# HGRN2 and RG-LRU layer: masked score copies over 64 rows, and two copies given to ACT

## The chip, the cores and the metric

One core of a Trainium2 chip runs the whole kernel. The metric is the device time of one execution in microseconds. The engines are named as in the profile: PE (TensorE, matmuls) with its weight loads PEld, DVE (VectorE), ACT (ScalarE), POOL (GpSimd) and SP (SyncE, which issues the transfers).

## The reference

One layer of a hybrid decoder over 2048 tokens of width 1024, all in float32. After an RMS norm, one input projection feeds two mixers side by side: HGRN2 (4 heads, 128x128 state each, chunks of 32 tokens) and RG-LRU (width 512). Their outputs are concatenated and projected back; then come a SwiGLU feed-forward part (inner width 2816) and a last RMS norm. The parts that the change touches are these:

```python
def step(state, xs):                       # HGRN2, one chunk of 32
    q_, k_, lg, v_ = xs
    b = jnp.cumsum(lg, axis=-2)
    q_dec = q_ * jnp.exp(b)
    k_dec = k_ * jnp.exp(-b)
    scores = jnp.where(causal, jnp.einsum('bhtk,bhsk->bhts', q_dec, k_dec), 0.0)
    o = jnp.einsum('bhts,bhsv->bhtv', scores, v_) + jnp.einsum('bhtk,bhkv->bhtv', q_dec, state)
    k_state = k_ * jnp.exp(b_last - b)
    new_state = jnp.exp(b_last)[..., 0, :, None] * state + jnp.einsum('bhsk,bhsv->bhkv', k_state, v_)
...
log_a = -LRU_C * r * jax.nn.softplus(-a_param)      # RG-LRU
a = jnp.exp(log_a)
b_in = jnp.sqrt(-jnp.expm1(2.0 * log_a)) * (ig * xc)
```

## The kernel before

The tokens go through in two halves of 1024, and each half in two column blocks (c = 0, 1) of 512. Every float32 operand of a large matmul is split into a high and a low part, and a product is three matmuls (high by high, low by high, high by low). The high part is made by ACT, the low part by DVE.

For each half there is first the projection of the values (`pv`), then eight steps s, then the gate projection (`pg`), the output projection (`poh`), and later the feed-forward part (`quad`, `pda`, `pdb`). A step s takes two slices of the input projection, computes them for both column blocks by 24 matmuls each (`pa`, `pb`, lines 234 to 236), and is of the HGRN2 kind where s is even (one head) and of the RG-LRU kind where s is odd. So a half has 8 HGRN2 units and 8 RG-LRU units, the whole kernel 16 of each, in pairs: two HGRN2 units, two RG-LRU units, and so on.

A HGRN2 unit has three parts.

- `hg_pre` (lines 252 to 319) takes `pa` and `pb` and prepares the decayed queries and keys. On ACT: two sigmoids (lines 254, 255), a logarithm (257), exponentials (262, 278 to 280). On DVE: a scan over each chunk (259) and some twenty products, of which lines 310, 315 and 318 are among the last. 128 tokens are treated as one block of four chunks of 32.
- `hg_mid` (322 on) is put behind the next unit's `pa`. PE transposes the state keys into the bank `pk` (329), DVE copies them to `kut` (331), PE forms the scores of each block in the bank `pc` (337), rows 0 to 63 by the columns 0 to 127 and rows 64 to 127 by the columns 64 to 127. The scores are copied to `sct`, a tile that was zeroed once and whose lower triangle stays zero: on the diagonal 32x32 pieces by DVE, under a mask (`keep`, 349), right of them by ACT (351). PE then forms the state update `pu` from `kut` (354), and DVE adds it to the states (359).
- `hg_post` is put behind the unit after that: PE forms the outputs `po` from the states (371) and from the scores (372), ACT sums their squares (377), POOL takes the power -0.5 (379), and DVE scales (380).

A RG-LRU unit has `lru_pre` (copy, GELU on ACT at 391, a convolution on DVE at 397 and 401, the split at 207 and 208) and `lru_post`: PE forms the two gates `pr` and `pi` (411 to 413), ACT their sigmoids (416, 417), a tanh (419) and the decay `r` by Exp (420); DVE squares `r` into `xc` (422) and combines it with the tanh (423), ACT takes the root (424), and DVE goes on with a product (425), the scan (426) and the gating (428). The next step's weights are split in between (163, 164).

Tiles come from pools with few slots. The banks `pk`, `pc`, `pu`, `po`, `pr` and `pi` share four of the eight PSUM banks; `kut`, the states `S` and the gates' tiles share the five slots of `late`.

The order of the work on each engine is not written out by hand. The program says what depends on what, and with

```python
with tile.TileContext(nc, schedule_with_timeline_sim=True) as tc:
```

a planner puts all instructions into one queue for each engine when the program is built, with a model of the instructions' times. On the chip each engine takes its queue in order. The loads of activation tables on ACT (`ACT_TABLE_LOAD` in the profile) are put in ahead of the functions that need them.

Of the kernel before, what the change touches and what calls it, by code (L numbers as in the profile page):

```python
# [10 lines left out]
AF = mybir.ActivationFunctionType  # L11
ALU = mybir.AluOpType

P = 128
# [11 lines left out]
TPC = CW // P  # L26
NTT = T // P
SUB = 32
# [7 lines left out]
def hybrid_layer(ctx: ExitStack, tc: tile.TileContext, x, x_t, norm_w, cols, w_in, gate_w, w_out, w_gu, w_down, out):  # L36
    nc = tc.nc
    const = ctx.enter_context(tc.tile_pool(name="const", bufs=1))
# [24 lines left out]
    def late(nm):  # L63
        return sb.tile([P, CW], F32, tag="late", name=nm, bufs=5)
# [4 lines left out]
    def aux(nm):  # L69
        return psp.tile([P, CW], F32, tag="aux", name=nm)  # L70
# [4 lines left out]
    mask = const.tile([P, CW], mybir.dt.bfloat16, name="mask")  # L75
    nc.gpsimd.memset(mask, 1.0)
    nc.gpsimd.memset(mask.rearrange("p (n s) -> p n s", s=SUB)[:, :, 0:1], 0.0)

    keep = const.tile([P, SUB], mybir.dt.uint8, name="keep")
    tri = sb.tile([P, CW], F32, tag="pg", name="tri", bufs=16)  # L80
    nc.gpsimd.memset(tri, 1.0)
    nc.gpsimd.affine_select(
        out=tri[:, 0:P], in_=tri[:, 0:P], pattern=[[1, P]], compare_op=ALU.is_ge, fill=0.0, base=0, channel_multiplier=-1
    )
    for j in range(4):
        nc.gpsimd.tensor_copy(out=keep[j * SUB : (j + 1) * SUB], in_=tri[j * SUB : (j + 1) * SUB, j * SUB : (j + 1) * SUB])
    sc_t = []
    for i in range(2):
        s = const.tile([P, TPC, P], F32, name=f"sct{i}")
# [8 lines left out]
    v = nc.vector  # L98
# [225 lines left out]
    def hg_mid(h, c, st, vt, nm):  # L324
        hs = slice(h * P, (h + 1) * P)
        W, Wy, K, KU, G = (st[k] for k in ("W", "Wy", "K", "KU", "G"))
        pk = aux("pk" + nm)
        for n in range(TPC):
            nc.tensor.transpose(out=pk[:, n * P : (n + 1) * P], in_=KU[:, n * P : (n + 1) * P], identity=ident)
        kut = late("kut" + nm)  # L330
        v.tensor_copy(out=kut, in_=pk)

        pc = aux("pc" + nm)
        for n in range(TPC):
            o = n * P
            for r0, w in ((0, W), (2 * SUB, Wy)):
                nc.tensor.matmul(
                    pc[r0 : r0 + 2 * SUB, o + r0 : o + P],
                    lhsT=K[:, o + r0 : o + r0 + 2 * SUB],
                    rhs=w[:, o + r0 : o + P],  # L340
                    start=True,
                    stop=True,
                )
        sc = sc_t[flip[0] % 2]
        flip[0] += 1
        pc4 = pc.rearrange("p (n t) -> p n t", t=P)
        for j in range(4):
            rows, cs = slice(j * SUB, (j + 1) * SUB), slice(j * SUB, (j + 1) * SUB)
            v.copy_predicated(out=sc[rows, :, cs], mask=keep[rows].unsqueeze(1).broadcast_to([SUB, TPC, SUB]), data=pc4[rows, :, cs])
            if j < 3:  # L350
                nc.scalar.copy(out=sc[rows, :, (j + 1) * SUB : P], in_=pc4[rows, :, (j + 1) * SUB : P])
        pu = aux("pu" + nm)
        for n in range(TPC):
            nc.tensor.matmul(pu[:, n * P : (n + 1) * P], lhsT=kut[:, n * P : (n + 1) * P], rhs=vt[:, n, hs], start=True, stop=True)

        S = late("S" + nm)
        states = [carry[:, c % 2, h, :]] + [S[:, n * P : (n + 1) * P] for n in range(TPC - 1)] + [carry[:, 1 - c % 2, h, :]]
        for n in range(TPC):
            v.scalar_tensor_tensor(
                out=states[n + 1], in0=states[n], scalar=G[:, n, 3:4], in1=pu[:, n * P : (n + 1) * P], op0=ALU.mult, op1=ALU.add  # L360
            )
        st["S"], st["sc"] = states, sc
# [22 lines left out]
    def lru_pre(u, psx, psg, nm):  # L385
        xp = sb.tile([P, CW + 4], F32, tag="pg", name="xp" + nm, bufs=16)
        v.tensor_copy(out=xp[:, 0:3], in_=hist[:, u, :])
        nc.scalar.copy(out=xp[:, 3 : 3 + CW], in_=psx)
        nc.gpsimd.tensor_copy(out=hist[:, u, :], in_=xp[:, CW : CW + 3])
        gl = page("gl" + nm)  # L390
        nc.scalar.activation(out=gl, in_=psg, func=AF.Gelu_apprx_tanh)
        xc = page("xc" + nm)

        def cw(k):
            return par[:, C_CONVW + k * 4 + u : C_CONVW + k * 4 + u + 1]

        v.tensor_scalar(
            out=xc, in0=xp[:, 0:CW], scalar1=cw(0), scalar2=par[:, C_CONVB + u : C_CONVB + u + 1], op0=ALU.mult, op1=ALU.add
        )
        for k in range(1, 4):  # L400
            v.scalar_tensor_tensor(out=xc, in0=xp[:, k : k + CW], scalar=cw(k), in1=xc, op0=ALU.mult, op1=ALU.add)
        xh, xl = page("xh" + nm, dt=F32R), page("xl" + nm, dt=F32R)
        split((xh, xl), xc)
        return gl, xc, xh, xl


    def lru_post(u, gl, xc, xh, xl, y, nm):
        pr, pi = aux("pr" + nm), aux("pi" + nm)
        for m, pg in enumerate((pr, pi)):
            gs = slice((m * NU + u) * P, (m * NU + u + 1) * P)  # L410
            nc.tensor.matmul(pg, lhsT=gwh[:, gs], rhs=xh, start=True, stop=False)
            nc.tensor.matmul(pg, lhsT=gwl[:, gs], rhs=xh, start=False, stop=False)
            nc.tensor.matmul(pg, lhsT=gwh[:, gs], rhs=xl, start=False, stop=True)
        r, ig, t = late("r" + nm), late("ig" + nm), late("t" + nm)
        us = slice(u, u + 1)
        nc.scalar.activation(out=r, in_=pr, func=AF.Sigmoid, bias=par[:, C_BA + u : C_BA + u + 1])
        nc.scalar.activation(out=ig, in_=pi, func=AF.Sigmoid, bias=par[:, C_BX + u : C_BX + u + 1])

        nc.scalar.activation(out=t, in_=r, func=AF.Tanh, scale=msp[:, us])
        nc.scalar.activation(out=r, in_=r, func=AF.Exp, scale=nmsp[:, us])  # L420
        v.tensor_tensor(out=ig, in0=ig, in1=xc, op=ALU.mult)
        v.tensor_tensor(out=xc, in0=r, in1=r, op=ALU.mult)
        v.scalar_tensor_tensor(out=t, in0=xc, scalar=1.0, in1=t, op0=ALU.add, op1=ALU.mult)
        nc.scalar.activation(out=t, in_=t, func=AF.Sqrt)
        v.tensor_tensor(out=ig, in0=ig, in1=t, op=ALU.mult)
        v.tensor_tensor_scan(out=t, data0=r, data1=ig, initial=hst[:, us], op0=ALU.mult, op1=ALU.add)
        nc.gpsimd.tensor_copy(out=hst[:, us], in_=t[:, CW - 1 : CW])
        v.tensor_tensor(out=y[:, u, :], in0=t, in1=gl, op=ALU.mult)
# [508 lines left out]
    for half in range(2):  # L937
# [36 lines left out]
        for s in range(8):  # L974
            i = s // 2
            ws.ahead(2)
            wa, wb = ws.take(2)
            ws.ahead(2)
            for c in range(NC):
                nm = f"{half}_{s}_{c}"  # L980
                pa = feat_mm(wa, xt[c], "pa" + nm)
                run_pending()
                pb = feat_mm(wb, xt[c], "pb" + nm)
                if s % 2 == 0:
                    st = hg_pre(i, pa, pb, nm)
                    nxt = [
                        lambda i=i, st=st, c=c, nm=nm: hg_mid(i, c, st, vts[c], nm),
                        lambda i=i, st=st, c=c, nm=nm: hg_post(i, st, vts[c], nm),
                    ]
                else:  # L990
                    r = lru_pre(i, pa, pb, nm)
                    nxt = [lambda i=i, r=r, c=c, nm=nm: lru_post(i, *r, ys[c], nm)]
                pend.append(nxt)
# [178 lines left out]
```

## Time and profile before

| | |
|---|---|
| median of 3 runs | 2132.01 us (2129.33 to 2132.49) |
| the profiled execution, from first to last instruction | 2131.1 us |
| PE busy | 2101.2 us (99%) |
| PEld busy | 1735.7 us (81%) |
| DVE busy | 1493.1 us (70%) |
| ACT busy | 1010.2 us (47%) |
| POOL busy | 82.2 us (4%) |
| mean granted clock of PE | 0.997 |

Of the profiled execution its span is known; the runs' times stand beside it, and the median is 0.9 us longer than the span. In the profile's rows L349 is line 349 of the kernel. A group's row gives engine, operation, what it writes and reads, shape and count, then busy time in us and the mean ns of one, then the idle time of the engine just before these instructions and what ended it. A row of the timeline gives start and length in us, and in brackets the idle time before it and its releaser. A busy share is an average over stages: a wait must be looked for in its own stage.

### The profile page before, as it was taken

What the parts mean: (1) busy time and instruction counts of PE and PEld (TensorE: products, weight loads), DVE (VectorE), ACT (ScalarE), POOL (GpSimd) and SP (SyncE); (2) the same over time, 40 slices, a digit from 0 to 9 for tenths busy, and PEclk for the clock granted to TensorE, in tenths of its full rate; (3) what the DMA queues carried; (4) which work ended last, traced back from release to release, by engine and by line L of the source; (5) the groups of instructions that cost most, each with busy time, mean ns of one, the idle gap of its engine ahead of it and who ended that gap; (6) DMA issues with size and microseconds to landing.
All of it is one profiled execution on the core that took longest, in us unless ns stands there. A gap on an engine that the chain in (4) does not pass through costs nothing.

```text
span 2131.1 us, 26161 instructions
## 1 busy us (share of the span) xinstructions
PE 2101.2 (99%) x9704; PEld 1735.7 (81%) x9704; DVE 1493.1 (70%) x2415; ACT 1010.2 (47%) x1647; POOL 82.2 (4%) x130
## 2 busy tenths in 40 slices
PE   8999999999999999999999999999999999999998
PEld 6887888888878888788888888888888888888887
DVE  6577664645776566877667669878867667669787
ACT  5577764535777644533333334335433333334333
POOL 2000001100000000000000000000000000000000
PEclk9999999999999999999999999999999999999999
DMA  6111104852111058433323257346423223257424
GB/s 216 61 40 40 40 20 160 282 162 69 31 39 40 20 174 260 156 112 99 106 93 129 89 187 253 109 136 205 143 94 119 95 90 123 94 206 252 156 88 143
DMA packets 138420, 262.84 MB, mean 123 GB/s; under 512 B 11186, under 2 KB 27570, under 8 KB 138292
## 3 DMA queue, kind: packets, MB, share of 16 engines
q1 hardware_dynamic: 138292, 261.17, 36.5%
q8 instruction: 76, 1.25, 0.2%
q14 instruction: 52, 0.43, 0.1%
HBM read 197.95 MB, written 63.18 MB: 123 GB/s over the span
## 4 chain that ended last, share of the span: by engine, by line
PE 83%; ACT 6%; DVE 5%; DMA 3%; issue 2%; SPq 0%; POOL 0%; DVEq 0%; POOLq 0%; ACTq 0%
PE quad_e L614 11%; PE quad_g L614 11%; PE quad_a L614 11%; PE pda L885 10%; PE pdb L885 6%; PE quad_f L614 5%; PE poh L246 2%; PE poh L247 2%; PE poh L248 2%; PE pb L236 2%; PE pb L234 2%; PE pb L235 2%; PE pa L234 1%; PE pa L235 1%; PE pg L248 1%
## 5 line engine op out<-in xcount | busy, mean ns | idle before, releaser
L614 PE MATMUL quad_f<-act_f,wgu_f 128*128 128x512 f32 x528 | 127.4, 389 | 1.8 <-DVE h L1050 1.7
L614 PE MATMUL quad_a<-act_a,wgu_a 128*128 128x512 f32 x528 | 127.5, 389 | 0.0
L614 PE MATMUL quad_g<-act_d,wgu_d 128*128 128x512 f32 x528 | 127.0, 389 | 0.2 <-DVE u L498 0.2
L614 PE MATMUL quad_g<-act_g,wgu_g 128*128 128x512 f32 x528 | 127.1, 390 | 0.0
L614 PE MATMUL quad_a<-act_b,wgu_b 128*128 128x512 f32 x528 | 127.1, 389 | 0.0
L614 PE MATMUL quad_e<-act_e,wgu_e 128*128 128x512 f32 x528 | 127.0, 389 | 0.0
L614 PE MATMUL quad_e<-act_c,wgu_c 128*128 128x512 f32 x528 | 126.9, 389 | 0.0
L614 PEld LDWEIGHTS quad_f<-act_f,wgu_f 128*128 128x128 f32 x528 | 99.0, 188 | 23.1 <-ACT act_g L207 2.1
L498 DVE TENSOR_TENSOR u<-u,quad_g 128x512 f32<-128x512 f32 x88 | 60.5, 687 | 80.9 <-PE quad_g L614 80.9
L614 PEld LDWEIGHTS quad_g<-act_d,wgu_d 128*128 128x128 f32 x528 | 99.0, 188 | 21.1 <-DVE u L498 0.6
L614 PEld LDWEIGHTS quad_e<-act_c,wgu_c 128*128 128x128 f32 x528 | 99.1, 188 | 20.6
L614 PEld LDWEIGHTS quad_g<-act_g,wgu_g 128*128 128x128 f32 x528 | 99.0, 188 | 20.8 <-DVE wgu_g L208 0.3
L614 PEld LDWEIGHTS quad_e<-act_e,wgu_e 128*128 128x128 f32 x528 | 99.0, 188 | 20.6
L614 PEld LDWEIGHTS quad_a<-act_b,wgu_b 128*128 128x128 f32 x528 | 99.0, 188 | 20.5
L614 PEld LDWEIGHTS quad_a<-act_a,wgu_a 128*128 128x128 f32 x528 | 98.9, 188 | 20.6 <-ACT act_c L207 0.2
L234 PE MATMUL pa<-xn,whi_in 128*128 128x512 f32 x256 | 101.7, 397 | 0.0
L236 PE MATMUL pb<-xn,whi_in 128*128 128x512 f32 x256 | 101.0, 395 | 0.0
L235 PE MATMUL pb<-xn,wlo_in 128*128 128x512 f32 x256 | 101.0, 394 | 0.0
L234 PE MATMUL pb<-xn,whi_in 128*128 128x512 f32 x256 | 100.9, 394 | 0.0
L235 PE MATMUL pa<-xn,wlo_in 128*128 128x512 f32 x256 | 100.6, 393 | 0.0
L236 PE MATMUL pa<-xn,whi_in 128*128 128x512 f32 x256 | 100.5, 393 | 0.0
L248 PE MATMUL poh<-whi_o,mx 128*128 128x512 f32 x256 | 99.9, 391 | 0.0
(331 smaller groups left out, 4940.9 us busy)
## 6 DMA issues: line engine op xcount, KB each, us to landing
raw<-in_w_gu SPq DMA_DIRECT2D x88, 512.0 KB, 3.8
raw_in<-in_w_in SPq DMA_DIRECT2D x48, 512.0 KB, 3.5
ao_p<-as SPq DMA_DIRECT2D x76, 256.0 KB, 2.6
raw_o<-in_w_out SPq DMA_DIRECT2D x32, 512.0 KB, 4.4
x<-in_x SPq DMA_DIRECT2D x32, 256.0 KB, 5.8
xrh<-in_x SPq DMA_DIRECT2D x32, 256.0 KB, 3.9
h<-h SPq DMA_DIRECT2D x32, 256.0 KB, 3.5
hn<-hths SPq DMA_DIRECT2D x32, 256.0 KB, 3.3
```

What stands on the lines that cost most here:

```text
L234: nc.tensor.matmul(ps, lhsT=whi[:, ks], rhs=hi, start=(k == 0), stop=False)
L235: nc.tensor.matmul(ps, lhsT=wlo[:, ks], rhs=hi, start=False, stop=False)
L236: nc.tensor.matmul(ps, lhsT=whi[:, ks], rhs=lo, start=False, stop=(k == KT - 1))
L246: nc.tensor.matmul(ps, lhsT=hi, rhs=whi[:, ks], start=(k == 0), stop=False)
L247: nc.tensor.matmul(ps, lhsT=hi, rhs=wlo[:, ks], start=False, stop=False)
L248: nc.tensor.matmul(ps, lhsT=lo, rhs=whi[:, ks], start=False, stop=(k == KT - 1))
L498: (e or v).tensor_tensor(out=out, in0=a, in1=b, op=op)
L614: nc.tensor.matmul(ps, lhsT=w[:, s, ks], rhs=x, start=first and k + n == 0, stop=k == 3 and n == 2, skip_group_check=not first)
L885: nc.tensor.matmul(ps, lhsT=x, rhs=y, start=first and q + n == 0, stop=q == gr.n - 1 and n == 2, skip_group_check=not first)
```

## The change

The mask `keep` is now the whole triangle of 128 columns, made by one cast on POOL in place of four. The scores are copied by two masked copies on DVE, over the rows 0 to 63 (128 columns of each of the four blocks) and 64 to 127 (the last 64 columns of each); the copies on ACT are gone. The copy of the transposed keys `kut` moves from DVE to ACT, and so does the square of the decay in `lru_post`, as the activation Square.

```diff
-    keep = const.tile([P, SUB], mybir.dt.uint8, name="keep")
+    keep = const.tile([P, P], mybir.dt.uint8, name="keep")
...
-    for j in range(4):
-        nc.gpsimd.tensor_copy(out=keep[j * SUB : (j + 1) * SUB], in_=tri[j * SUB : (j + 1) * SUB, j * SUB : (j + 1) * SUB])
+    nc.gpsimd.tensor_copy(out=keep, in_=tri[:, 0:P])
...
-        v.tensor_copy(out=kut, in_=pk)
+        nc.scalar.copy(out=kut, in_=pk)
...
-        for j in range(4):
-            rows, cs = slice(j * SUB, (j + 1) * SUB), slice(j * SUB, (j + 1) * SUB)
-            v.copy_predicated(out=sc[rows, :, cs], mask=keep[rows].unsqueeze(1).broadcast_to([SUB, TPC, SUB]), data=pc4[rows, :, cs])
-            if j < 3:
-                nc.scalar.copy(out=sc[rows, :, (j + 1) * SUB : P], in_=pc4[rows, :, (j + 1) * SUB : P])
+        for r0 in (0, 2 * SUB):
+            rows = slice(r0, r0 + 2 * SUB)
+            v.copy_predicated(
+                out=sc[rows, :, r0:P],
+                mask=keep[rows, r0:P].unsqueeze(1).broadcast_to([2 * SUB, TPC, P - r0]),
+                data=pc4[rows, :, r0:P],
+            )
...
-        v.tensor_tensor(out=xc, in0=r, in1=r, op=ALU.mult)
+        nc.scalar.activation(out=xc, in_=r, func=AF.Square)
```

## The prediction

> **What bounds the kernel now.** I read the page first: the span and the busy times.
>
> ```profile
> span 2131.1 us, 26161 instructions
> ...
> PE 2101.2 (99%) x9704; PEld 1735.7 (81%) x9704; DVE 1493.1 (70%) x2415; ACT 1010.2 (47%) x1647; POOL 82.2 (4%) x130
> ```
>
> PE is busy in all but 29.9 us of the span, and the change touches no matmul. So only two things can move the end: pauses of PE, and the granted clock after a pause. The second view is therefore the list of what PE waited for; its columns are total us, times, and the longest.
>
> ```profile
> PE pk L329 <- DVE lg L315: 6.5, 3, 2.9
> ...
> PE pu L354 <- DVE kut L331: 3.8, 2, 1.9
> ...
> PE po L372 <- DVE sct L349: 0.9, 2, 0.5
> ```
>
> These three rows, 11.2 us, are all the waiting that belongs to the HGRN2 steps, and each is a wait for DVE. The third view is the table by stretches: first the sum over the two stretches in which the units with these steps run (80 to 330 us and 490 to 720 us), then the ten microseconds around the four long pauses. The numbers are length, then busy time of PE, PEld, DVE, ACT, POOL, then the granted clock.
>
> ```profile
> sum 480.00, PE 468.71 PEld 389.44 DVE 337.49 ACT 341.68 POOL 36.08; mean PE 234.36 PEld 194.72 DVE 168.74 ACT 170.84 POOL 18.04
> ```
>
> ```profile
> 200.00:210.00 10.00, 7.13 (x38) 5.29 (x38) 9.96 (x30) 8.20 (x12) 0.19 (x1) 0.83 0.32 107
> 260.00:270.00 10.00, 8.09 (x53) 6.36 (x53) 8.70 (x21) 8.54 (x13) 0.71 (x1) 1.00 0.17 56
> ...
> 620.00:630.00 10.00, 7.94 (x42) 6.44 (x43) 9.97 (x33) 6.97 (x10) 0.19 (x1) 0.83 0.32 107
> 680.00:690.00 10.00, 8.07 (x33) 6.67 (x34) 8.64 (x27) 7.56 (x12) 1.34 (x2) 0.83 0.14 52
> ```
>
> The reader is to see that DVE and ACT are both about 70% busy there (337 and 342 of 480 us): neither is the engine with room to spare. Three of the four pauses are followed by a clock of 0.83, which is 10 x 0.17 = 1.7 us more each, 5.1 us together. All that can be won is 11.2 + 5.1 = 16.3 us, 0.8% of the time.
>
> The fourth view is the timeline ahead of the pause at 203.76, one engine after the other.
>
> ```profile
> 171.59 0.60 ACT L391 ACTIVATE gl<-pb 128x512 f32<-128x512 f32 x1 [6.55 <-PE pb L236]
> ...
> 179.18 0.72 ACT L420 ACTIVATE r<-r,tinies 128x512 f32<-128x512 f32 x1
> ...
> 188.26 0.72 ACT L420 ACTIVATE r<-r,tinies 128x512 f32<-128x512 f32 x1
> 189.00 1.28 ACT L255 ACT_TABLE_LOAD   x1
> ...
> 192.21 0.81 ACT L257 ACTIVATE lg<-sf,tinies 128x512 f32<-128x512 f32 x1
> ...
> 206.72 0.63 ACT L262 ACTIVATE eb<-b 128x512 f32<-128x512 f32 x1 [0.81 <-DVE b L259]
> ```
>
> ```profile
> 189.02 0.69 DVE L422 TENSOR_TENSOR xc<-r 128x512 f32<-128x512 f32 x1 [1.89 <-ACT r L420]
> ...
> 193.06 0.55 DVE L258 TENSOR_SCALAR sf<-sf,tinies 128x512 f32<-128x512 f32 x1 [2.62 <-ACT lg L257]
> ...
> 203.19 0.43 DVE L315 TENSOR_TENSOR lg<-nx,G 128x256 f32<-128x256 f32 x1
> ...
> 203.76 0.63 PE L329 MATMUL pk<-ident,lg 128*128 128x128 f32 x4 [2.87 <-DVE lg L315]
> ```
>
> From 171.59 to 206.72 ACT waits for nobody: 35 us on end. DVE, ten microseconds before the pause, sits idle for 1.89 and 2.62 us because ACT is late, and only then runs full up to L315. So the pause that is booked on DVE begins as lateness of ACT.
>
> **The change part by part.** Durations are from these groups (busy time, mean ns of one, idle before).
>
> ```profile
> L349 DVE COPY_PREDICATED sct<-keep,pc 32x128 f32<-32x128 uint8 x64 | 18.9, 296 | 6.6 <-ACT sct L351 5.4
> ...
> L422 DVE TENSOR_TENSOR xc<-r 128x512 f32<-128x512 f32 x16 | 11.1, 691 | 18.9 <-ACT r L420 18.9
> ...
> L380 DVE TENSOR_TENSOR v<-po,oss 128x512 f32<-128x512 f32 x16 | 11.0, 688 | 1.6 <-POOL oss L379 1.4
> ...
> L331 DVE COPY kut<-pk 128x512 f32<-128x512 f32 x16 | 10.9, 683 | 0.2
> ...
> L310 DVE TENSOR_TENSOR QI<-W,eB 128x256 f32<-128x256 f32 x16 | 6.7, 421 | 0.2
> ...
> L303 DVE TENSOR_TENSOR eb<-sq,nx 128x128 f32<-128x128 f32 x16 | 4.6, 285 | 0.1
> ```
>
> ```profile
> L424 ACT ACT_TABLE_LOAD x16 | 20.5, 1283 | 0.3
> ...
> L1033 ACT COPY hths<-tp_hs 128x512 f32<-128x512 f32 x32 | 17.6, 586 | 15.7 <-PE tp_hs L222 15.7
> L351 ACT COPY sct<-pc 32x384 f32<-32x384 f32 (+2 forms) x48 | 17.4, 362 | 35.2 <-DVE sct L349 35.2
> ...
> L424 ACT ACTIVATE t<-t 128x512 f32<-128x512 f32 x16 | 10.1, 633 | 1.9 <-DVE t L423 1.8
> ```
>
> Masked copies. Four of 296 ns and three ACT copies of 362 ns become two DVE copies over 64 rows, of 512 and 256 elements a row. A masked copy over 128 elements costs what a product over 128 costs (296 beside 285), so I let it grow as the products do: 296 + (688 - 285) = 699 ns and 296 + (421 - 285) = 432 ns, 1.13 us for 1.18 us, and DVE gains 16 x 0.05 = 0.8 us. Were the part that grows twice as dear, the pair would cost 1.67 us and DVE would lose 16 x 0.49 = 7.8 us; nothing excludes that. ACT loses 17.4 us of copies, and the 35.2 us for which its queue stood behind the masked copies. What stood behind them is the next unit's work on ACT (the conv input copy, the gelu), and the first fence of the timeline shows that ACT afterwards waits 6.55 us for PE before the long run begins: those 35.2 us lie ahead of ACT's slack, not inside the late run, and I cost their end at nothing. If that slack were not there, each pair of units would begin its run up to 2.2 us (35.2 / 16) earlier. The two waits of po for the scores, 0.9 us, I take as gone, since one queue now writes them without handing over.
>
> Transposed keys. The copy leaves DVE (16 x 0.683 = 10.9 us) for ACT (16 x 0.586 = 9.4 us). It waits for PE's transposes pk; behind it in ACT's queue stand the next unit's sigmoid, logarithm and exponentials, and PE's pu waits for it. Where it comes in ACT's queue decides. This is the pause at 268.15:
>
> ```profile
> 243.24 0.62 ACT L207 CAST xh<-xc 128x512 fp32r<-128x512 f32 x1 [0.82 <-DVE xc L401]
> ...
> 254.05 0.71 ACT L420 ACTIVATE r<-r,tinies 128x512 f32<-128x512 f32 x1
> ...
> 260.29 0.61 PE L329 MATMUL pk<-ident,lg 128*128 128x128 f32 x4
> ...
> 261.88 1.04 ACT L163 CAST whi_in<-raw_in 128x1024 fp32r<-128x1024 f32 x1
> ...
> 266.80 0.63 ACT L262 ACTIVATE eb<-b 128x512 f32<-128x512 f32 x1 [0.45 <-DVE b L259]
> ...
> 266.81 0.69 DVE L263 TENSOR_TENSOR lg<-b 128x512 f32<-128x512 f32 x1
> ...
> 267.41 0.68 DVE L331 COPY kut<-pk 128x512 f32<-128x512 f32 x1
> ...
> 268.15 1.16 PE L354 MATMUL pu<-v,kut 128*128 128x128 f32 x8 [1.91 <-DVE kut L331]
> ```
>
> pk is done at 260.90, but DVE's queue has the copy behind L263. On ACT it can come right after the cast that ends at 262.92; then it is done at 263.5 and the wait is gone: -1.9 us, and -3.8 us with its twin at 686. Or it comes behind L262, as it now comes behind L263, which starts at the same instant; with the Square (below) ahead it is then done at about 268.6, 0.5 us later than now: +1.0 us for both. The order of DVE's queue speaks for the late place, ACT's freedom at 262.92 for the early one; no row decides, and I take one of each, -1.4 us. Both ends stay in the range.
>
> Squared decay. It leaves DVE (11.1 us) for ACT at 0.63 us, by the row of the other 128x512 activation from SBUF to SBUF: 16 x 0.633 = 10.1 us. It goes right behind the Exp of L420. That line stands twice in the run that ends in the pause at 203.76, and DVE's L422, which it relieves, was idle time on either side. So L255, L257 and L258 come 2 x 0.63 = 1.26 us later, and so does pk. At 622 the same order stands: +2.5 us for both. Ahead of 268.15 the run begins at 243.24 and holds one Exp; its 0.63 us is in the numbers above.
>
> [...]
>
> The mask itself is built once on POOL, one cast for four, in the first microseconds, where the next POOL instruction waits for DVE: nothing, and at most the length of one such cast. No DMA is added or moved.
>
> Sum: DVE -0.8 - 10.9 - 11.1 = -22.8 us, ACT -17.4 + 9.4 + 10.1 = +2.1 us, and on PE's path +2.5 - 1.4 - 0.9 = +0.2 us. The third pk wait (6.5 less 2 x 2.9, 0.7 us) I leave as it is: a key copy goes from ahead of it, a Square comes. The clock's three dips I leave too. The profiled span becomes 2131.3 us. The median of the runs shown, 2132.01, is 0.9 us above the profiled span; so 2132.2 us, and I say 2132: no change. About 0.2%, 4.3 us, is what a measurement of this kernel can tell from none.
>
> **The rivals.** Faster: the plan of the queues is made anew. DVE is full (9.96 and 9.97 of 10 us) right ahead of two pauses and sheds 0.68 + 0.69 = 1.37 us for each pair of units. If that arrives in front of pk, the four pauses shrink by 4 x 1.37 = 5.5 us and one dip of 1.7 us goes: 2132 - 7.2 = 2125. The ceiling is 2132 - 16.3 = 2116. For it: every wait of PE names DVE. Against it: DVE's own idle ahead of that run, on ACT.
>
> Slower, by one mechanism: PE's order. The plan sees a lighter DVE and puts pk, and with it pu, up to 1.37 us earlier into PE's stream, while the real ACT, with its table loads between nearly all functions, is no earlier. PE then stands still for what it would have done in between: 4 x 1.37 = 5.5 us, and the pause at 268, the one without a dip, gets one of 1.7 us: 2132 + 7.2 = 2139. It decides from the point where the waits for pk and pu together pass 11.2 + 4.3 = 15.5 us. For it: at 203.76 and 268.15 PE already stands at work that its order has put too early for the real ACT. Against it: the plan may equally move pk back.
>
> [...]
>
> The edit does not do what it says: Square after Exp may need another table. Then 16 loads of 1.283 us (20.5 us) come in, two in each late run: 4 x 2 x 1.28 = 10.2 us, 2142. Against it: the Squares of lines 377 and 774 have no load of their own. But none of them follows an Exp.
>
> **How the numbers follow.** No change to speak of 0.37; faster by the rival 0.35; slower by the order 0.24, by the table 0.04. So faster 0.35, same 0.37, slower 0.28. For 8 in 10 the range must reach the middles of both neighbours: 2121, past the 2125 and toward the ceiling, to 2142, past the 2139 and the dear masked copies. The likeliest case alone is 2128 to 2136, from both places of the key copy and the Square with and without room.
>
> **What would show it.** In the changed profile: two masked copies of about 0.70 and 0.43 us on a unit; no ACT copies of scores; kut on ACT at 0.59 us; a Square at 0.63 us behind each L420 and no more than the loads of now; waits of pk around 3.5 us each; waits of pu for kut gone in about half; none of po for the scores. I am wrong if pk's waits shrink (DVE was the cause after all), if new waits of PE for kut on ACT appear, or if the table loads in the two stretches rise in number.

## The result, and the profile after

The changed kernel takes 2148.03 us (median of 4 runs, 2147.11 to 2149.27), the kernel before 2132.25 us beside it (4 runs, 2129.33 to 2133.12). The ratio is 1.0079, with a 95% interval of 1.0065 to 1.0093: slower by 16 us. The profiled execution has a span of 2147.6 us, 16.5 us more than that of before.

The busy times of the profile page:

```profile
span 2147.6 us, 26096 instructions
...
PE 2103.7 (98%) x9704; PEld 1738.0 (81%) x9704; DVE 1473.6 (69%) x2351; ACT 1012.0 (47%) x1633; POOL 83.7 (4%) x127
```

DVE has 19.5 us less to do, ACT 1.8 us more, and PE has the same 9704 matmuls. The gain in work is there, and PE still waits more. What PE waits for (total us, times, longest):

```profile
PE pk L328 <- DVE lg L314: 20.5, 6, 5.3
...
PE tp_o L221 <- DVE v L1003: 3.8, 2, 1.9
...
PE po L373 <- DVE sct L348: 1.2, 2, 0.6
```

The waits of pk have gone from 6.5 to 20.5 us, a wait at the end of each half is new (3.8), the wait of pu for the key copy is gone. Together 25.5 us, against 11.2. The four long waits end at 209, 271, 634 and 697 us. The stretches around them (length, busy PE, PEld, DVE, ACT, POOL, then the granted clock) and the sum over the two stretches in which these units run:

```profile
200.00:210.00 10.00, 5.50 (x25) 4.10 (x23) 7.26 (x19) 8.75 (x10) 0.30 (x1) 0.96 0.19 57
...
260.00:270.00 10.00, 5.38 (x24) 4.13 (x22) 8.48 (x22) 9.90 (x12) 0.30 (x1) 1.00 0.17 54
270.00:280.00 10.00, 9.33 (x66) 7.90 (x67) 9.81 (x32) 5.73 (x9) 1.07 (x1) 0.83 0.14 53
...
630.00:640.00 10.00, 5.92 (x29) 4.70 (x30) 9.96 (x30) 7.88 (x11) 1.38 (x2) 0.66 0.18 54
...
690.00:700.00 10.00, 4.69 (x27) 3.43 (x26) 9.08 (x23) 9.04 (x13) 0.30 (x1) 0.69 0.33 106
```

```profile
sum 480.00, PE 456.39 PEld 379.29 DVE 311.05 ACT 330.54 POOL 37.61; mean PE 228.20 PEld 189.64 DVE 155.53 ACT 165.27 POOL 18.80
```

PE has lost 12.3 us in the 480 us (468.71 before). The clock dips more: adding 10 x (1 - clock) over all ten-microsecond rows of the two stretches gives 10.3 us, against 5.1 us before. Waits and dips together rise from 16.3 to 35.8 us, by 19.5 us. That is more than the 16.5 us of the span; the rest of the span is 3.0 us shorter, and why is not traced. The loss lies in the waits and dips.

The prices of the new instructions (busy time, mean ns of one, idle before):

```profile
L348 DVE COPY_PREDICATED sct<-keep,pc 64x512 f32<-64x512 uint8 x16 | 11.6, 722 | 0.8 <-PE pc L336 0.7
...
L423 ACT ACTIVATE xc<-r 128x512 f32<-128x512 f32 x16 | 10.0, 625 | 0.2
L330 ACT COPY kut<-pk 128x512 f32<-128x512 f32 x16 | 9.5, 594 | 0.0
```

They are what they were taken for, and the Square has no table load of its own: L423 stands 16 times among ACT's rows, with no row of loads beside it. So it is not the price of the parts. The timeline shows what it is. At about 244 us, ACT's queue begins on the next HGRN2 unit. Before:

```profile
245.17 0.60 ACT L254 ACTIVATE sq<-pa 128x512 f32<-128x512 f32 x1
...
247.57 0.82 ACT L257 ACTIVATE lg<-sf,tinies 128x512 f32<-128x512 f32 x1
248.41 1.28 ACT L416 ACT_TABLE_LOAD   x1
249.70 0.69 ACT L416 ACTIVATE r<-pr,par 128x512 f32<-128x512 f32 x1
...
254.66 0.62 ACT L280 ACTIVATE lg<-lg 128x512 f32<-128x512 f32 x1
```

After:

```profile
244.80 0.60 ACT L253 ACTIVATE sq<-pa 128x512 f32<-128x512 f32 x1
...
245.94 1.28 ACT L425 ACT_TABLE_LOAD   x1
247.23 0.63 ACT L425 ACTIVATE t<-t 128x512 f32<-128x512 f32 x1
247.88 1.28 ACT L417 ACT_TABLE_LOAD   x1
249.18 0.69 ACT L417 ACTIVATE r<-pr,par 128x512 f32<-128x512 f32 x1
...
251.56 1.28 ACT L421 ACT_TABLE_LOAD   x1
252.85 0.72 ACT L421 ACTIVATE r<-r,tinies 128x512 f32<-128x512 f32 x1
253.59 1.28 ACT L256 ACT_TABLE_LOAD   x1
254.89 0.82 ACT L256 ACTIVATE lg<-sf,tinies 128x512 f32<-128x512 f32 x1
...
259.75 1.28 ACT L425 ACT_TABLE_LOAD   x1
261.04 0.63 ACT L425 ACTIVATE t<-t 128x512 f32<-128x512 f32 x1
...
264.25 0.62 ACT L279 ACTIVATE lg<-lg 128x512 f32<-128x512 f32 x1
```

```profile
270.67 1.09 PE L328 MATMUL pk<-ident,lg 128*128 128x128 f32 x4 [5.29 <-DVE lg L314]
```

The two runs start 0.4 us apart. Before, the logarithm of the HGRN2 unit comes first and the gates (L416) and the decay of the second RG-LRU unit behind it. After, a root, the gates and the decay (L421) of the RG-LRU units stand ahead of the logarithm, each with its table load, and another root with its load stands between the exponentials: the logarithm is 7.3 us later, the last exponential 9.6 us, and pk 10.4 us (260.29 before). The planner has put ACT's queue in another order. The second passage, at 200 us, has changed too: from the start of the logarithm to the start of the last exponential it takes 5.4 us before, where the root stands ahead of all the exponentials, and 8.2 us after, where it stands among them. I call the one order "log first", the other "gates first" (the decay of the second unit ahead of the logarithm). A half has three passages from RG-LRU to HGRN2 units, at about 140, 200 and 260 us, and both halves have the same orders. Before has gates first at the second passage alone, after at the second and third.

### The profile page after: what moved, and what is told of

It reads as the page before. It is cut to its first block, busy times and chain, and to the rows that moved or that the text cites. A ratio compares the mean times of both kernels' runs of the same rounds, so it can differ in the third digit from the quotient of the medians.

```text
span 2147.6 us, 26096 instructions
## 1 busy us (share of the span) xinstructions
PE 2103.7 (98%) x9704; PEld 1738.0 (81%) x9704; DVE 1473.6 (69%) x2351; ACT 1012.0 (47%) x1633; POOL 83.7 (4%) x127
## 4 chain that ended last, share of the span: by engine, by line
PE 87%; ACT 6%; DVE 4%; DMA 2%; issue 1%; SPq 0%; POOL 0%; DVEq 0%; POOLq 0%; ACTq 0%
PE quad_e L615 11%; PE quad_g L615 11%; PE quad_a L615 11%; PE pda L886 10%; PE pdb L886 7%; PE quad_f L615 5%; PE poh L246 3%; PE poh L247 3%; PE poh L245 3%; PE pb L235 2%; PE pb L234 2%; PE pb L233 2%; PE pa L233 2%; PE pa L235 2%; PE pa L234 2%
## 5 line engine op out<-in xcount | busy, mean ns | idle before, releaser
L615 PEld LDWEIGHTS quad_a<-act_b,wgu_b 128*128 128x128 f32 x528 | 99.0, 188 | 20.5
L246 PE MATMUL poh<-wlo_o,mx 128*128 128x512 f32 x256 | 100.0, 394 | 0.1
```

Source lines behind the costliest of these rows:

```text
L246: nc.tensor.matmul(ps, lhsT=hi, rhs=wlo[:, ks], start=False, stop=False)
L615: nc.tensor.matmul(ps, lhsT=w[:, s, ks], rhs=x, start=first and k + n == 0, stop=k == 3 and n == 2, skip_group_check=not first)
```

## The experiments

Every kernel is planned anew when it is built, so an edit or a set order on one engine can move the orders of the others as well. To set an order I added `tc.add_manual_dep(later, earlier, ORDER)`, a dependency of the class NoSync between two instructions of one engine: it is there to tell the planner which comes first. The table holds every kernel: its ratio to runs of before made beside it, then for the profiled execution the waits of pk, of pu for kut, and of po and tp_o, the dips (worked out as above), the span less all of these, and at how many of the three passages the gates come first.

| kernel | ratio (95%) | span | pk | pu | po, tp_o | dips | rest | gates first |
|---|---|---|---|---|---|---|---|---|
| before | 1 | 2131.1 | 6.5 | 3.8 | 0.9 | 5.1 | 2114.8 | 1 |
| after | 1.0079 (1.0065 to 1.0093) | 2147.6 | 20.5 | 0 | 5.0 | 10.3 | 2111.8 | 2 |
| e1 | 1.0033 (1.0022 to 1.0044) | 2136.1 | 16.1 | 0 | 1.4 | 6.8 | 2111.8 | 2 |
| e2 | 1.0058 (1.0043 to 1.0073) | 2143.5 | 16.0 | 0 | 3.3 | 10.3 | 2113.9 | 2 |
| e3 | 1.0052 (1.0037 to 1.0067) | 2140.2 | 16.1 | 0 | 4.2 | 8.5 | 2111.4 | 2 |
| e4 | 1.0010 (1.0001 to 1.0020) | 2130.7 | 6.5 | 5.3 | 2.0 | 0 | 2116.9 | 0 |
| e5 | 1.0033 (1.0020 to 1.0046) | 2139.1 | 1.6 | 8.0 | 6.0 | 5.1 | 2118.4 | 0 |
| e6 | 1.0030 (1.0019 to 1.0041) | 2136.1 | 1.9 | 12.5 | 1.2 | 5.1 | 2115.4 | 0 |
| e7 | 1.0107 (1.0090 to 1.0124) | 2156.7 | 20.1 | 0 | 5.1 | 17.0 | 2114.5 | 3 |
| e8 | 1.0035 (1.0022 to 1.0048) | 2135.7 | 13.9 | 0 | 3.3 | 3.4 | 2115.1 | 3 |
| e9 | 0.9986 (0.9977 to 0.9995) | 2125.8 | 1.9 | 1.8 | 7.2 | 0 | 2114.9 | 0 |
| e10 | 1.0017 (1.0008 to 1.0027) | 2130.7 | 2.0 | 8.4 | 4.4 | 1.7 | 2114.2 | 0 |
| e11 | 1.0020 (1.0010 to 1.0029) | 2134.8 | 6.4 | 10.0 | 0 | 0 | 2118.4 | 0 |
| e12 | 0.9987 (0.9977 to 0.9996) | 2125.2 | 3.6 | 6.9 | 0.5 | 0 | 2114.2 | 0 |
| e13 | 1.0035 (1.0022 to 1.0047) | 2139.0 | 16.0 | 0 | 1.4 | 10.2 | 2111.4 | 2 |
| e14 | 0.9994 (0.9985 to 1.0004) | 2128.7 | 0.5 | 5.2 | 5.6 | 1.7 | 2115.7 | 0 |

The rest stays between 2111.4 and 2118.4 us over spans that differ by 31.5 us: waits and dips are most of what moves. The scatter of 7 us in the rest is not explained, so a difference of a few microseconds between two kernels can't be read from the waits alone.

### e1: the root out of the way

After, with the root of the second RG-LRU unit behind the last exponential of the next HGRN2 unit:

```diff
+        last_exp = nc.scalar.activation(out=lg, in_=lg, func=AF.Exp)
+        if h > 0 and nm.endswith("_0"):
+            tc.add_manual_dep(roots[-1].ins, last_exp.ins.name, ORDER)
...
+        roots.append(nc.scalar.activation(out=t, in_=t, func=AF.Sqrt))
```

> The changed kernel with one order pinned: in ACT's queue the root of the second RG-LRU unit (line 425) stands behind the last exponential of the HGRN2 unit after it (line 279), with no wait added. In the changed kernel the planner put this root, with two table loads, between the exponentials of that unit at two of the three passages of each half. Order theory (the 16 us come from where the planner put the root): the exponentials end 3 to 4 us earlier, pk's waits for DVE fall from 20.5 us to between 5 and 13 us, time 2133 to 2141 us. Load theory (the Square and the key copy make ACT late wherever they stand): pk's waits stay above 17 us, time 2145 to 2149 us.

Measured: 2138.31 us, ratio 1.0033, inside the range of the order theory. An edit of order alone takes back more than half of the loss, and the waits of tp_o go. But pk's waits only fall to 16.1 us, where 5 to 13 were expected: the two passages keep the gates ahead of the logarithm. The root between the exponentials is a part of it, not the whole.

### e2, e3, e4: the parts

e2 is before with the Square alone; e3 is after with the key copy back on DVE; e4 is after with the old masked copies and score copies.

```diff
e2, to before:
-        v.tensor_tensor(out=xc, in0=r, in1=r, op=ALU.mult)
+        nc.scalar.activation(out=xc, in_=r, func=AF.Square)
e3, to after:
-        nc.scalar.copy(out=kut, in_=pk)
+        v.tensor_copy(out=kut, in_=pk)
e4, to after:
-        for r0 in (0, 2 * SUB):
...
+        for j in range(4):
...
+            if j < 3:
+                nc.scalar.copy(out=sc[rows, :, (j + 1) * SUB : P], in_=pc4[rows, :, (j + 1) * SUB : P])
```

> Before, with only the square of the decay moved to ACT. ACT's order at the two bad passages is that of the kernel before, with the Squares put in, and no root stands between exponentials. Order theory: pk's waits near those of before (6.5 us, at most 9), time 2130 to 2135 us. Load theory: the Squares are the larger part of what ACT's late run took on, so about half of the loss or more, 2139 to 2144 us.

> The changed kernel with the key copy back on DVE: masked copies over 64 rows and the Square on ACT. Here the planner puts the root between the exponentials only at the third passage of each half (steps 5 to 6), not at the second (3 to 4). Order theory: two waits of pk of 4 to 5.5 us, at the third passages, and small ones at the second; in all 9 to 14 us, time 2137 to 2143 us. Load theory: the passages are alike, each with one wait of the same size; time as with the Square alone within 2 us.

> The changed kernel with the old masked copies and ACT's score copies: key copy and Square on ACT. No root stands between exponentials; pk stands 5 to 19 matmuls earlier in PE's order than in the kernel before. Order theory as told of the root: no wait of pk over 4 us, time 2130 to 2138 us. Load theory: both additions are on ACT, and the score copies too, so at least as slow as the changed kernel, 2147 to 2155 us. The prediction's rival (pk too early in PE's order): waits of pk at all three passages, 10 to 15 us in all, 2136 to 2142 us.

Measured: 2144.72, 2142.94 and 2132.93 us. The Square alone costs 0.6%, yet with the Square and the key copy together, and thus with the most work on ACT of the kernels so far (1026.3 us busy), e4 loses only 0.1%. That fells the theory of the load in its plain form, for which e4 was to be the worst. My first theory, that only the root's place among the exponentials counts, falls as well. e2 is slow, slower than both ranges given, with its roots ahead of the exponentials and none among them; it was expected to keep ACT's order of before, and it did not. And e3 has the root among them at the third passages alone, yet its four waits of pk are alike, 4.0 to 4.1 us each. The waits of e2, then of e4:

```profile
PE pk L329 <- DVE lg L315: 16.0, 6, 4.1
```

```profile
PE pk L329 <- DVE lg L315: 6.5, 6, 1.1
PE pu L354 <- ACT kut L331: 5.3, 6, 0.9
...
PE po L372 <- DVE sct L349: 2.0, 6, 0.3
```

e4 has many small waits and no dip, and what it has in common with none of the slow kernels is that its plan has the log first at all three passages. The Square by itself turns the third passage from log first to gates first, as the whole change does. That gave the theory that the rest was to test: the order of the queue decides, and the edits count by the order that they bring about.

### e5 and e7: the same edits, the other order

e5 is the complete change with log first at all passages; e7 is e4 with gates first.

```diff
e5, to after:
+        log = nc.scalar.activation(out=lg, in_=sf, func=AF.Ln, scale=omlb[:, h : h + 1], bias=lb[:, h : h + 1])
+        if h > 0 and nm.endswith("_0"):
+            tc.add_manual_dep(gates[-1].ins, log.ins.name, ORDER)
...
+        gates.append(nc.scalar.activation(out=r, in_=pr, func=AF.Sigmoid, bias=par[:, C_BA + u : C_BA + u + 1]))
e7, to e4:
+        sig = nc.scalar.activation(out=sf, in_=psf, func=AF.Sigmoid)
+        if h > 0 and nm.endswith("_0"):
+            tc.add_manual_dep(sig.ins, decays[-1].ins.name, ORDER)
...
+        decays.append(nc.scalar.activation(out=r, in_=r, func=AF.Exp, scale=nmsp[:, us]))
```

> The changed kernel complete, with one dependency of order added and no arithmetic changed: at each of the passages from an RG-LRU step to an HGRN2 step, the gates of the second RG-LRU unit stand behind the logarithm of the HGRN2 unit in ACT's queue (the order that the kernel without the masked copies has by itself). Theory of the order: the four waits of pk for DVE of 4.5 to 5.3 us and their clock dips go, no wait of pk stays above 1.5 us, 2128 to 2136 us. Theory of the load (what the parts cost on ACT, wherever they stand): the Squares and the key copies are all still there, so 2144 us or more with pk waits of 16 us or more in sum.

> The kernel with the key copy and the Square on ACT but the old masked copies and score copies, which took 2132.9 us, now with the opposite dependency of order: the sigmoid ahead of the HGRN2 logarithm stands behind the decay exponential of the second RG-LRU unit, as it does in the changed kernel. Theory of the order: waits of pk of 3 to 5 us come back at the four passages, most with a clock dip, 2138 to 2148 us. Theory that the masked copies themselves are what costs: nothing comes back, 2131 to 2135 us.

Measured: 2139.71 us for e5 and 2155.78 us for e7. e7 shows the order without a change in what is computed: from 1.0010 to 1.0107. Its waits and two rows of its clock:

```profile
PE pk L333 <- DVE lg L319: 16.6, 4, 4.3
...
PE tp_o L222 <- DVE v L1006: 3.9, 2, 1.9
PE pk L333 <- ACT eb L266: 3.5, 2, 1.8
```

```profile
210.00:220.00 10.00, 8.50 (x43) 6.90 (x43) 8.61 (x31) 6.06 (x12) 1.08 (x1) 0.66 0.16 54
...
270.00:280.00 10.00, 7.10 (x33) 5.64 (x34) 9.68 (x34) 6.96 (x11) 1.08 (x1) 0.66 0.14 53
```

That is slower than expected (2138 to 2148): all four long waits here bring a dip of 3.4 us, two shorter waits one of 1.7 us, and the first passages have waits of pk as well (3.5 us). The order of the key copy moves with the gates in e7, but no wait of pu is left.

e5 takes back 8 us by its time, 0.46% by its ratio, and no pk wait over 0.3 us is left, as expected. But it stays at 1.0033, and its time lies between the two theories, 3.7 us above the one and 4.3 us below the other:

```profile
PE pu L359 <- ACT kut L334: 8.0, 6, 1.3
PE po L377 <- DVE sct L352: 6.0, 6, 1.0
PE pk L332 <- DVE lg L318: 1.6, 6, 0.3
```

The waits of pk are gone and new ones of pu and po stand in their place. In e4 the key copy stands ahead of the next unit's exponentials, in e5 behind three of them and their table load.

### e6, e8, e12: the Square and the kernel before in set orders

e6 is e2 with e5's dependency, e12 is before with it, e8 is before with e7's.

> The kernel before with the Square alone on ACT, and the same dependency of order: the gates of the second RG-LRU unit behind the logarithm of the HGRN2 unit. Theory of the order: 2128 to 2136 us, pk waits under 6 us in sum. Theory of the load: the Square lengthens ACT's run ahead of the logarithm wherever it stands, so it stays at 2141 us or more, with pk waits near the 16.0 us of the Square alone.

> The kernel before with nothing changed but the order: the sigmoid ahead of the HGRN2 logarithm behind the decay exponential of the second RG-LRU unit at every passage. Before has this order at one passage of three, with a pk wait of 2.9 us. Theory of the order: waits of 3 to 4 us at four or more places, 2136 to 2146 us, with none of the three edits made. Theory of the load: with Square and key copy on DVE ACT is no later than before, so 2130 to 2135 us.

> The kernel before with nothing changed but the order: the gates of the second RG-LRU unit behind the logarithm of the HGRN2 unit at every passage (before has this at one passage of three). Theory of the order: the three pk waits of before (6.5 us) and their dips go, but the key copy, on DVE, comes behind the scan as in e6, with pu waits of about 2 us: 2130 to 2140 us. Theory of the load, by which order is nothing: 2130 to 2134 us with the waits of before.

Measured: 2138.42, 2138.21 and 2127.70 us. e8 and e12 have none of the three edits: the set order, with the plan that it brings, moves the kernel before by +0.35% and by -0.13%. e8 lies in its range, with waits a little shorter than expected; e12 lies below both of its ranges: no wait of pk is longer than 1.1 us and no dip is left. Their waits, e8 first:

```profile
PE pk L333 <- DVE lg L319: 13.9, 8, 2.9
...
PE po L376 <- DVE sct L353: 3.3, 2, 1.7
```

```profile
PE pu L358 <- DVE kut L335: 6.9, 6, 1.9
...
PE pk L333 <- DVE lg L319: 3.6, 4, 1.1
```

PE's own order does not explain e8: the first pk of its third passage stands behind as many of the large matmuls as in before, within 2, and PE waits 2.9 us for it, where before, with log first there, has no wait.

e6 missed: its pk waits are gone (1.9 us), but the six waits of pu for the key copy, on DVE here, are 12.5 us where e12 has 6.9, with three dips. With log first at every passage, the Square still costs 0.4% by e6 against e12. PE's order puts pu a few matmuls earlier in e6, too, so what the Square does through its length and what it does through the plan isn't told apart there.

### e9 and e13: the place of the key copy

e9 is e5 with the exponentials of the next HGRN2 unit behind the key copy; e13 is after with that dependency alone.

```diff
+        exp = nc.scalar.activation(out=eb, in_=b, func=AF.Exp)
+        if nm.endswith("_1"):
+            tc.add_manual_dep(exp.ins, keys[-1].ins.name, ORDER)
...
+        keys.append(nc.scalar.copy(out=kut, in_=pk))
```

> The changed kernel complete, with the order of e5 (second gates behind the logarithm) and one more dependency of order: the exponentials of the HGRN2 unit of the second tile of tokens stand behind the key copy of the first, as they do in the kernel without the masked copies. Theory of the order, now in two places: the six pu waits of 1.3 us for the key copy (8.0 us in e5) fall under 1 us each, and with them the dips; 2129 to 2136 us. Theory that the change has a cost of its own beside the order (load, masked copies): it stays at 2139 us or more, as in e5.

> The changed kernel complete with the key copy's order alone (the exponentials of the second tile's HGRN2 unit behind the key copy of the first); the gates and the logarithm are left as they are planned, and at two of three passages the second gates stand ahead of the logarithm. If the gates' order carries its part by itself: pk waits of 3 to 5 us at four places, 2136 to 2146 us. If the key copy's order carries all of it: 2126 to 2132 us.

Measured: 2128.04 us for e9, ratio 0.9986 (0.9977 to 0.9995), and 2137.83 us for e13. ACT's timeline in e5 and then in e9, from the logarithm on:

```profile
207.01 0.82 ACT L258 ACTIVATE lg<-sf,tinies 128x512 f32<-128x512 f32 x1
207.85 1.28 ACT L265 ACT_TABLE_LOAD   x1
...
210.73 0.56 ACT L334 COPY kut<-pk 128x512 f32<-128x512 f32 x1
```

```profile
206.30 0.81 ACT L258 ACTIVATE lg<-sf,tinies 128x512 f32<-128x512 f32 x1
207.02 0.56 ACT L336 COPY kut<-pk 128x512 f32<-128x512 f32 x1
207.60 1.28 ACT L265 ACT_TABLE_LOAD   x1
```

The copy runs 3.7 us earlier, 3.0 us of it against the logarithm, and the waits of pu fall from 8.0 to 1.8 us with no dip left; e9 comes out just below its expected range. So the whole change with two orders set is 0.9% faster than the change as it was planned (0.9986 / 1.0079). It also comes out 0.14% below before, with an interval that ends just under 1, and that is no more than the set order gives to the kernel before (e12, 0.9987).

e13 keeps four pk waits of 4.0 us, as the part of the gates would have it; set in e13, the order of the gates takes 0.49% (to e9), and in after 0.46% (to e5). What the key copy's place is worth is read from e5 and e9. It can't be read from after and e13, though the ratios seem to add up: after has no wait of pu to save. What e13 has less of is waits of pk and tp_o, and its plan has moved the root as well, out from among the exponentials to ahead of them. In e13, at the third passage:

```profile
254.80 0.63 ACT L429 ACTIVATE t<-t 128x512 f32<-128x512 f32 x1
...
256.75 0.63 ACT L263 ACTIVATE eb<-b 128x512 f32<-128x512 f32 x1
```

From the start of the logarithm to the start of the last exponential it takes 5.4 us there, and 9.4 us in after.

### e10, e11, e14: the other parts alone, and the masked copies' place

e10 is before with the masked copies alone, e11 with the key copy alone; both plans have the log first. e14 is e9 with the reverse differences (the subtraction behind the scan) of the next unit behind the two masked copies on DVE.

> The kernel before with the masked copies over 64 rows alone; keys and squares on DVE. In its planned order the second gates stand behind the logarithm at the passages. Theory of the order: no pk wait over 1.5 us, 2128 to 2138 us (the key copy is on DVE behind the scan there, so pu waits of up to 2.2 us as in e6 are possible). Theory that the masked copies themselves cost: 2140 us or more.

> The kernel before with the transposed keys copied by ACT alone. In its planned order the second gates stand behind the logarithm, but the key copy behind the exponentials, as in e5. Theory of the order: no pk wait over 1.5 us, pu waits of about 1.3 us six times, 2130 to 2140 us. Theory that the key copy by itself costs nothing: 2128 to 2133 us.

> The kernel of e9 with one more dependency of order, on DVE: the reverse differences (the subtraction behind the scan) of the second tile's HGRN2 unit stand behind the two masked copies of the first, 0.69 us of DVE's work. If the place makes the wait: the six po waits of 7.2 us shrink by about 6 x 0.6 us, 2122 to 2128 us. If the differences were needed at once: the pk waits grow by as much, 2126 to 2130 us.

Measured: 2133.75, 2135.20 and 2129.92 us. Each with the plan that it got, the masked copies alone cost 0.17% and the key copy alone 0.20% (0.30% and 0.33% against e12, which has the log first as they do). Both have new waits of pu; the waits of pk fall to 2.0 us in e10 and stay at 6.4 us in e11, in shorter pieces. Neither is free and neither is the loss of 0.8%. e14 missed its first range, and lies in the second by its time but not by the waits of pk that this one named: in its plan po waits 5.6 us in place of 7.2, but pu waits 5.2 in place of 1.8, since the plan now asks for pk and pu seven matmuls earlier at two passages:

```profile
PE po L381 <- DVE sct L356: 5.6, 6, 0.9
PE pu L363 <- ACT kut L338: 5.2, 6, 0.9
```

## Why the prediction was wrong

The forecast was 2132 us; it is 2148. The step that failed stands in the part on the squared decay, "So L255, L257 and L258 come 2 x 0.63 = 1.26 us later, and so does pk", and in the sum, "I leave as it is" of the third pk wait and "The clock's three dips I leave too". All three keep ACT's queue as it was and put the new instructions in between. The edit had the queue planned anew, and the new order put three table loads and six activations more between the first sigmoid and the logarithm of the third passage, and a root with its loads among the exponentials: the last exponential came 9.6 us later and pk 10.4 us, where I had taken the 0.63 us of one Square. In place of the +0.2 us of the sum, the waits grew by 14.3 us and the dips by 5.2 us. Point by point:

- PE as the bound, moved only by its pauses and the clock: right in the main. The rest in the table is constant within 7 us over all kernels. The ceiling that I gave (2116) was not reached by any; the best are at 2128.
- The pause booked on DVE begins as lateness of ACT: right, and more so after, where DVE waits for the logarithm for 38.9 us in all, of 31.4 before. The rows of DVE's waits, before and after:

```profile
DVE sf L258 <- ACT lg L257: 31.4, 12, 6.9
```

```profile
DVE sf L257 <- ACT lg L256: 38.9, 12, 6.9
```

- Prices: masked copy of 512 a row at 699 ns, measured 722; key copy 586, measured 594; Square 633, measured 625. DVE lost 19.5 us of the 22.8, ACT gained 1.8 of the 2.1. The sum of work was right and said nothing of the time.
- The key copy's place decides: right where the gates' order is set, and of more weight than my -3.8 to +1.0 us: e5 and e9 differ by 0.0047, some 10 us; waits of pu are 6.2 us and dips 5.1 us less, and the waits of po and pk 1.5 us more. In the changed kernel the copy came late at all passages, behind the last exponential, and still the wait of pu is gone at all of them, where I had said about half.
- The two waits of po for the scores, taken as gone: 1.2 us of them stay, and in e9 they are the largest that is left, 7.2 us.
- "A table of its own" for the Square: no load stands ahead of L423. My last sign, that the table loads in the two stretches would rise in number, hardly shows: in the first stretch (80 to 330 us) they number 54 before and 55 after, in the whole execution 115 and 117, and e9, faster than before, has 117 too. It isn't their number but what they stand ahead of.
- The rival on the slower side gave 2139, and its threshold (waits of pk and pu over 15.5 us) was passed. But its mechanism is not what happened: pk was to come earlier in PE's order. It comes later there: ahead of each of the two late pk of the first half, PE runs 14 more of the large matmuls (pv, pa, pb) after than before. The planner did put pk later; the real pk was later still, by the 4.5 and 5.3 us that PE waits there. The "plan made anew" I had as the rival on the faster side; it was made anew, to the worse.
- The dips, in the sum left at 5.1 us, are 10.3 us after: behind each of the four long waits of pk, 4.50 to 5.31 us, stands one of 1.7 or 3.4 us. The last section has what the runs show.

## What to carry to other kernels

Where a planner sets the queues, a small edit is also a throw for a new order: compare the order of each engine's queue ahead of the longest waits before any sum of durations, and where a good order is known, set it by a dependency and compare the edits on equal orders. On ACT's queue here, with its 111 to 119 table loads of 1.283 us, what stood ahead of the one result that PE waited for counted, not how much work the queue held: e4 and e7 make the same edits, with 1026.3 and 1029.0 us of work on ACT, and their ratios are 1.0010 and 1.0107. A saving on an engine that only feeds the bound one showed no gain here: with its two orders set, the changed kernel, with 19 us less DVE work, came out within 0.01% of the kernel before with its one order set (0.9986 and 0.9987). Whether before would gain from a set key copy too was not run.

## What the runs showed of the hardware

Dips of the clock followed long pauses here, not the sum of the waits: e4 has 13.8 us of waits in 18 pieces of at most 1.1 us, e11 16.4 us in pieces of at most 1.8 us, and neither has a dip; after has 25.5 us with pieces up to 5.3 us and 10.3 us of dips. In the two stretches each of the 22 pauses of 3.7 us or more (3.75 to 5.31 us, in after, e1, e2, e3, e7 and e13) has a dip of 1.7 or 3.4 us behind it; e7 has 0.66 in the row behind a wait of 4.25 us. Of the pauses between 1.7 and 3.0 us some have one and some don't, and the longer ones not more surely: e8 has a dip after 2.20 us in both halves and none after 2.94 and 2.92 us (PE's idle time in the rows from 200, 620, 260 and 680 us). Where two shorter pauses stand close together (1.3 and 1.0 us in e5, 0.9 and 0.9 in e14) a dip follows at some of the places and not at others. What decides in these cases stays open.

The dips come out at about 1.7 us (0.83 of a ten-microsecond row, as in before) or 3.4 us (0.66, as in e7), where a dip over two rows is added up. Not every dip has a pause of 3.7 us or more ahead of it: before has one behind 2.87 us. What ties the size of a dip to its pause was not shown: in after 1.7 us stand behind 5.29 us and 3.4 us behind 4.50 us.

Fewer table loads were not faster by themselves. Summed over the rows of ACT, the kernels have 111 to 119 loads of 1.283 us each, and the number does not sort them: those with 117 run from 2127.70 us (e12) to 2155.78 us (e7), and e1, with the fewest, takes 2138.31 us. A queue with far fewer loads was not run. What counted was which loads stood ahead of the results that pk waits for.
